# A hybrid decoder layer on one core: the first input row sent together with its norms, block products grouped by tile shape, transposes in place of selecting products, and an output scaled by VectorE alone

## The chip, the cores and the metric

One Trainium2 chip, one core used. The time is device microseconds of one execution of the whole program. The engines run their own instruction streams side by side and wait for one another by semaphores: TensorE (PE for its matmuls, PEld for its weight loads in the profile), VectorE (DVE), ScalarE (ACT), GpSimd (POOL) and SyncE (SP). DMAs are issued by SP, ACT or POOL and carried out by 16 DMA engines that all three share.

## The reference

One step of a decoder layer for 288 tokens: a prompt of 256 and 8 samples of 4. The model width is 2048.

```
h = rms_norm(x, norm1)
z = h @ w_in          # q, k, v of both branches, gates
A: sliding-window attention (128), 16 q heads, 4 kv heads, with a sink
B: gated linear attention, 4 heads, key dim 256, value dim 512:
   prompt: o_t = sum over s <= t of (q_t . decay(s..t) . k_s) v_s, and the final state
   samples: the same, on top of a cached 256x512 state per sample and head
   o = rms_norm(o) * silu(z_r)
y = sigmoid(z_gs) * (o_A @ p_swa) + sigmoid(z_gg) * (o_B @ p_gla)
x = x + y @ w_o
x = x + square(relu(rms_norm(x, norm2) @ w_up)) @ w_down
return rms_norm(x, final_norm), new caches and states
```

## The kernel before, in words

Everything is held with features on the 128 partitions and the 288 tokens along the free axis, so x is 16 rows of 128x288 (a "row" below is one such 128x288 slice, 144 KB). Weights are read once, in chunks of 128x1024 (512 KB, 521 of them), each holding two halves of 128x512. Every product of a weight and an activation is made from three fp32r products of 128x288: high part by high part (L230), high part of the weight by low part of the activation (L231), low part of the weight by high part of the activation (L232). `wsplit` makes the two parts of a weight half: ACT casts it to `whi` (L208), DVE subtracts to get `wlo` (L155). Five `whi` and five `wlo` buffers let this run some two chunks ahead of PE; six `raw` buffers let SP load further ahead. A `gemm` of 512 output columns has four PSUM banks `mm` and runs over 8 chunks, 24 matmuls each.

**The first gemm, `kv`,** is the only one whose activations are made while it runs. `load_x` loads two rows of x per chunk (SP, L266 and L268), then ACT makes `hh` = x times norm1 (L270), DVE the low part `hl` (L271), and the squares of x for the norm are taken by ACT (chunks 1, 3, 5, 6, 7) or by POOL (chunks 0, 2, 4) and added into `acc1` by DVE or POOL (L152). The normalisation itself, `rstd1`, is applied to the gemm's output; `rsqrt_mean` gets it by summing `acc1` over partitions with the matmuls `ssq` (L240), then two ACT and four DVE operations. norm1 is part of the tile `norms` (26 KB), which POOL's queue sends (L166). Ahead of the first real matmul PE runs nine matmuls of 128x512 on a constant tile, `warm` (L302).

**The order of the work** on each engine comes from a scheduler that takes the program as written with its own idea of costs. Generators (`swa`, `gla`, `gla_sample`) are put into queues, and `pump` advances them by some pieces after every weight chunk, so that attention and the linear attention of one head lie between the chunks of the gemms.

**The prompt's linear attention** (`gla`) builds a 256x256 causal score matrix in one PSUM bank, `pa` (diagonal blocks of 128 at columns 0 to 127 and 256 to 383, the off-diagonal block between them). Decays are factored per block, so it is put together from one 128x128 product (`cross`, L652), two of 64x64 (L658), four of 32x32 next to the diagonal (L660) and eight of 32x32 on it (L663), each contracted over 128 partitions and made twice (t = 0 and 1), for each of 4 heads. All operands are f32, and the profile has two MATMUL records for each such product. The 64x64 products both go to PSUM partitions 0 to 63. `at` is the copy of `pa` in SBUF.

**The samples** (`gla_sample`) have their 512 outputs in four partial sums on the four groups of 32 partitions of `ob`. Four products with a 128x32 selecting matrix `ii` (L782) turn them and add the four; ACT copies the result into `og` (L783).

**The end.** After the last gemm, `rsqrt_mean` gives `rstd3`; the 16 rows of x1 are scaled by it in six pieces, four on DVE (1, 3, 4 and 3 rows) and two on POOL (2 and 3 rows) (L149), and sent to `y` by SP and ACT (L968). The two prompt states of the last head, `sp`, are made last (PE L692, ACT copy L694, SP DMA L695).

Of the kernel before, what the change touches and what calls it, by code (L numbers as in the profile page):

```python
# [130 lines left out]
def step_kernel(ctx: ExitStack, tc: tile.TileContext, a: dict):  # L131
# [80 lines left out]
    def gemm(name, xh, xl, evac, rate=(), first=None):  # L212
        nk = 2 * chunks_of(name)
        ps = [pmm.tile([P, 512], F32, name="mm", tag="mm") for _ in range(4)]
        for c in range(nk // 2):
# [2 lines left out]
            raw = main.tile([P, 1024], F32, name="raw", tag="raw", bufs=6)
            if FIRST[name] + c == 0:
                for s in range(2):  # L220
                    SY.dma_start(raw[:, 512 * s:512 * s + 512], a["w"][0, :, 512 * s:512 * s + 512])
# [4 lines left out]
            turns = c in (0, nk // 2 - 1)
            for i, m in [(i, m) for m in range(4) for i in range(2)] if turns else [(i, m) for i in range(2) for m in range(4)]:
                k, hi, lo = parts[i]
                o, sl = ps[m][:, :NT], slice(m * P, m * P + P)
                T.matmul(o, lhsT=hi[:, sl], rhs=xh(k), start=k == 0, stop=False)  # L230
                T.matmul(o, lhsT=hi[:, sl], rhs=xl(k), start=False, stop=False)  # L231
                T.matmul(o, lhsT=lo[:, sl], rhs=xh(k), start=False, stop=k == nk - 1)  # L232
                if k == nk - 1:
# [26 lines left out]
    acc1 = [main.tile([P, NT], F32, name=f"acc1{i}", tag=t) for i, t in ((0, "acc"), (1, "acc_b"))]  # L260

    def load_x(c):
        sl = slice(2 * c, 2 * c + 2)
        if c == 0:
            for k in range(2):
                SY.dma_start(xa[:, k], a["x"][:, k])  # L266
        else:
            SY.dma_start(xa[:, sl], a["x"][:, sl])  # L268
        for k in (2 * c, 2 * c + 1):
            S.mul(hh[:, k], xa[:, k], n1[:, k:k + 1])  # L270
            V.scalar_tensor_tensor(hl[:, k], xa[:, k], n1[:, k:k + 1], f(hh[:, k]), ALU.mult, ALU.subtract)  # L271
        sq = early.tile([P, 2, NT], F32, name="sq", tag="sq", bufs=3)
        odd = c in (1, 3, 5, 6, 7)
        if odd:
            S.activation(flat(sq), flat(xa[:, sl]), AF.Square)
# [292 lines left out]
    def gla(h):  # L568
# [36 lines left out]
        V.memset(pa[:, :384], 0.0)  # L605
        kds = []
        for t in range(2):
# [45 lines left out]
            if t == 0:  # L653
                cross()
            for blk in range(2):
                b0 = 256 * blk
# [1 line left out]
                T.matmul(pa[0:64, b0 + 64:b0 + P], lhsT=l64[:, 0:64], rhs=l64[:, 64:P], start=False, stop=False)  # L658
                for i in (0, 64):
                    T.matmul(pa[i:i + 32, b0 + i + 32:b0 + i + 64], lhsT=l32[:, i:i + 32],  # L660
                             rhs=l32[:, i + 32:i + 64], start=False, stop=False)
                for i in (0, 32, 64, 96):
                    T.matmul(pa[i:i + 32, b0 + i:b0 + i + 32], lhsT=en[:, blk, i:i + 32],  # L663
                             rhs=dg[:, i:i + 32], start=False, stop=False)
# [25 lines left out]
        def state(t, pst, tag="A"):  # L690
# [4 lines left out]
            SY.dma_start(a["sp"][h, t], so)  # L695
# [9 lines left out]
    def gla_sample(h):  # L705
# [75 lines left out]
        for j in range(4):  # L781
            T.matmul(pt[:, TS * j:TS * j + TS], lhsT=ob[:, P * j:P * j + P], rhs=ii, start=True, stop=True)  # L782
# [268 lines left out]
```

## Time and profile before

| | |
|---|---|
| runs | 1806.95, 1806.47, 1808.19 us (median 1806.95) |
| profiled execution: time, span | 1806.9 us, 1805.1 us |
| mean granted TensorE clock | 0.998 |
| PE, PEld, DVE, ACT, POOL busy | 1789.4, 1746.8, 1103.2, 855.8, 84.6 us |
| HBM read, written | 298.25 MB, 23.66 MB |

The span runs from the first to the last instruction of the profiled execution; 1.8 us of its time lie around it. "Busy" counts the time in which at least one instruction of the engine was in flight. Since matmuls are pipelined, neighbouring records overlap, and the pace of PE is read from the distance between the starts of two matmuls. A row of the timeline has start, duration, engine, line, operation, tiles, form and count, and in brackets the idle time ahead of it with what ended it.

### The profile page before, as it was taken

The numbers are of one execution on the slowest core, as the hardware profiler recorded it, in microseconds if no ns is written. First come the engines' busy times: TensorE is split into PE (matmuls) and PEld (weight loads), VectorE is DVE, ScalarE is ACT, GpSimd is POOL, SyncE is SP. The second block draws the span as 40 slices with busy tenths as digits, with TensorE's granted clock in tenths as the row PEclk, the third lists the DMA queues.
The fourth block names the chain that finished last, engine by engine and source line by source line (L and its number), as shares of the span: only waits on it lengthen the run. The fifth ranks groups of instructions, "written<-read, shape, count | busy, mean of one in ns | idle before, by whom it ended". The sixth has DMA issues, their size and how long they took to land.

```text
span 1805.1 us, 34198 instructions
## 1 busy us (share of the span) xinstructions
PE 1789.4 (99%) x13499; PEld 1746.8 (97%) x13499; DVE 1103.2 (61%) x2092; ACT 855.8 (47%) x1593; POOL 84.6 (5%) x97
## 2 busy tenths in 40 slices
PE   9999999999999999999999999999999999999997
PEld 8999998998999989999999999999999999999997
DVE  7886575685665767666666554455544554455544
ACT  5566464443453644554444553345433553345443
POOL 2000000100100101000123000000000000000002
PEclk9999999999999999999999999999999999999999
DMA  7734347557557466545554444544444444444452
GB/s 270 242 120 164 131 153 260 201 188 251 176 205 260 137 248 223 167 168 168 206 176 164 164 166 161 175 164 164 163 168 167 168 161 167 164 167 169 156 175 88
DMA packets 92177, 324.13 MB, mean 180 GB/s; under 512 B 11040, under 2 KB 12720, under 8 KB 92016
## 3 DMA queue, kind: packets, MB, share of 16 engines
q1 hardware_dynamic: 91584, 320.93, 51.1%
q8 instruction: 106, 1.74, 0.4%
q10 hardware_dynamic: 288, 0.74, 0.1%
q0 software_dynamic: 144, 0.28, 0.1%
q14 instruction: 55, 0.45, 0.1%
HBM read 298.25 MB, written 23.66 MB: 178 GB/s over the span
## 4 chain that ended last, share of the span: by engine, by line
PE 96%; DVE 2%; ACT 1%; issue 0%; DMA 0%; DVEq 0%; SPq 0%; ACTq 0%
PE mm L230 30%; PE mm L232 30%; PE mm L231 30%; PE pu L771 1%; PE pos L762 1%; DVE wlo L155 1%; PE pst L692 1%; PE score L379 0%; PE po L685 0%; DMA raw<-in_w 0%; PE pt L408 0%; PE ssq L240 0%; PE o L418 0%; DVE x L149 0%; ACT whi L208 0%
## 5 line engine op out<-in xcount | busy, mean ns | idle before, releaser
L155 DVE TENSOR_TENSOR wlo<-raw,whi 128x512 fp32r<-128x512 f32 x1040 | 721.4, 705 | 601.1 <-ACT whi L208 599.2
L208 ACT CAST whi<-raw 128x512 fp32r<-128x512 f32 x1040 | 631.7, 619 | 832.5 <-PE mm L231 782.0
L230 PE MATMUL mm<-hh,whi 128*128 128x288 f32 x1472 | 441.2, 300 | 1.2 <-ACT whi L208 0.6
L232 PE MATMUL mm<-hh,wlo 128*128 128x288 f32 x1472 | 434.1, 295 | 2.0 <-DVE wlo L155 1.8
L231 PE MATMUL mm<-hl,whi 128*128 128x288 f32 x1472 | 434.3, 295 | 0.0
L232 PE MATMUL mm<-h2h,wlo 128*128 128x288 f32 x1024 | 301.9, 295 | 0.0
L232 PE MATMUL mm<-uh,wlo 128*128 128x288 f32 x1024 | 301.9, 295 | 0.0
L230 PE MATMUL mm<-h2h,whi 128*128 128x288 f32 x1024 | 301.8, 295 | 0.0
L230 PE MATMUL mm<-uh,whi 128*128 128x288 f32 x1024 | 301.8, 295 | 0.0
L231 PE MATMUL mm<-h2l,whi 128*128 128x288 f32 x1024 | 301.6, 295 | 0.0
L231 PE MATMUL mm<-ul,whi 128*128 128x288 f32 x1024 | 301.6, 295 | 0.0
L230 PEld LDWEIGHTS mm<-hh,whi 128*128 128x128 f32 x1472 | 277.1, 188 | 6.0 <-issue 1.7
L232 PEld LDWEIGHTS mm<-hh,wlo 128*128 128x128 f32 x1472 | 276.8, 188 | 3.0 <-DVE wlo L155 2.7
L231 PEld LDWEIGHTS mm<-hl,whi 128*128 128x128 f32 x1472 | 277.2, 188 | 2.6 <-issue 0.7
L232 PEld LDWEIGHTS mm<-h2h,wlo 128*128 128x128 f32 x1024 | 192.3, 188 | 0.0
L232 PEld LDWEIGHTS mm<-uh,wlo 128*128 128x128 f32 x1024 | 192.3, 188 | 0.0
L231 PEld LDWEIGHTS mm<-ul,whi 128*128 128x128 f32 x1024 | 192.1, 188 | 0.1
L231 PEld LDWEIGHTS mm<-h2l,whi 128*128 128x128 f32 x1024 | 192.1, 188 | 0.1
L230 PEld LDWEIGHTS mm<-uh,whi 128*128 128x128 f32 x1024 | 192.0, 188 | 0.1
L230 PEld LDWEIGHTS mm<-h2h,whi 128*128 128x128 f32 x1024 | 192.0, 188 | 0.1
L232 PE MATMUL mm<-yh,wlo 128*128 128x288 f32 x256 | 75.5, 295 | 0.0
L232 PE MATMUL mm<-gh,wlo 128*128 128x288 f32 x256 | 75.4, 295 | 0.0
(274 smaller groups left out, 1823.0 us busy)
## 6 DMA issues: line engine op xcount, KB each, us to landing
raw<-in_w SPq DMA_DIRECT2D x519, 512.0 KB, 3.3
raw<-in_s SPq DMA_DIRECT2D x32, 512.0 KB, 3.7
out_ssn<-raw SPq DMA_DIRECT2D x32, 512.0 KB, 2.9
x<-in_x SPq DMA_DIRECT2D x4, 576.0 KB, 6.1
out_sp<-so SPq DMA_DIRECT2D x8, 256.0 KB, 2.7
x<-in_x SPq DMA_DIRECT2D x7, 288.0 KB, 8.1
kc<-in_kc SPq DMA_DIRECT2D x2, 512.0 KB, 7.0
out_kcn<-kc SPq DMA_DIRECT2D x2, 512.0 KB, 5.5
```

What stands on the lines that cost most here:

```text
L155: eng.tensor_tensor(out, x, y, ALU.subtract)
L208: S.copy(hi, raw)
L230: T.matmul(o, lhsT=hi[:, sl], rhs=xh(k), start=k == 0, stop=False)
L231: T.matmul(o, lhsT=hi[:, sl], rhs=xl(k), start=False, stop=False)
L232: T.matmul(o, lhsT=lo[:, sl], rhs=xh(k), start=False, stop=k == nk - 1)
L692: T.matmul(pst, lhsT=kdt[:, blk, P * t:P * t + P], rhs=vt[:, blk], start=blk == 0, stop=blk == 1)
L762: T.matmul(pos[r:r + 32], lhsT=qm[:, t, 32 * (b0 + g):32 * (b0 + g) + 32], rhs=st[g][:, 512 * t:512 * t + 512], start=b0 == 0, stop=b0 == ...
L771: T.matmul(pu, lhsT=km[:, P * t:P * t + P], rhs=vs, start=True, stop=True)
```

## The change

Five things change.

1. **norm1 travels with the first row of x.** A new tile `xn` (norm1 and row 0) is the first DMA of SP, row 1 the second. The first weight chunk is issued in two halves by ACT, ahead of its table load. The other constants (`norms` without norm1, `ident`, `bm`, `seg`) leave POOL's queue for SP's, behind the loads of the first gemm. In chunk 1 each row and each weight half is a DMA of its own.
2. **Order inside the first gemm.** ACT and DVE now treat each half of a chunk by itself: `hh`, `whi`, `hh`, `whi`, and the squares behind them. All squares are ACT's, all sums DVE's (one addition of 128x576 for each chunk but the first, whose squares are written to `acc1` directly); POOL does nothing there. PE takes the first half of chunk 0 as four high, four low-activation and four low-weight products instead of switching between both halves.
3. **Block products grouped by tile shape.** Both 64x64 products come first, the second one now on PSUM partitions 64 to 127 at columns 384 to 447 of `pa`; then the eight 32x32 on the diagonal, then the four beside it. A second, small ACT copy brings the moved block to its place in `at`; the memset of `pa` covers 448 columns.
4. **Transposes for the samples.** The four products with `ii` become four 128x128 transposes, and DVE adds the four partial sums with one reduction of 128x512 out of PSUM, in place of ACT's copy.
5. **The end.** The two `sp` copies and their DMAs (now on ACT's queue) are written ahead of the scaling; DVE alone scales x1, in ten pieces of 1, 1, 2, 2, 2, 2, 2, 2, 1 and 1 rows, and SP sends each.

```
-    G.dma_start(norms, a["norms"])
+    raw0 = main.tile([P, 1024], F32, name="raw", tag="raw", bufs=6)
+    for s in range(2):
+        S.dma_start(raw0[:, 512 * s:512 * s + 512], a["w"][0, :, 512 * s:512 * s + 512])
...
+            parts = []
+            for s in range(2):
+                if first is not None:
+                    first[1](2 * c + s)
+                parts.append((2 * c + s, *wsplit(raw[:, 512 * s:512 * s + 512])))
             if first is not None:
-                first(c)
...
+                first[2](c)
-            turns = c in (0, nk // 2 - 1)
+            turns = c == nk // 2 - 1 or c == 0 and first is None
...
+            if c == 0 and first is not None:
+                order[:12] = [(0, m, j) for j in range(3) for m in range(4)]
...
+    def weigh_x(k):
+        n1 = xn[0][:, k:k + 1]
+        S.mul(hh[:, k], x_row(k), n1)
+        V.scalar_tensor_tensor(hl[:, k], x_row(k), n1, f(hh[:, k]), ALU.mult, ALU.subtract)
+    def square_x(c):
         if c == 0:
+            acc1.append(early.tile([P, 2, NT], F32, name="acc1"))
             for k in range(2):
+                S.activation(acc1[0][:, k], x_row(k), AF.Square)
         else:
-        odd = c in (1, 3, 5, 6, 7)
-        if odd:
-            S.activation(flat(sq), flat(xa[:, sl]), AF.Square)
-        else:
-            mul(sq, xa[:, sl], xa[:, sl], G)
-        e, acc = (V, acc1[1]) if odd else (G, acc1[0])
...
+            S.activation(flat(sq), flat(xa[:, 2 * c:2 * c + 2]), AF.Square)
+            add(flat(acc1[0]), flat(acc1[0]), flat(sq))
...
+        xn.append(early.tile([P, KT + NT], F32, name="xn"))
+        SY.dma_start(xn[0], a["xn"])
+        SY.dma_start(xa[:, 1], a["x"][:, 1])
...
-    G.dma_start(ident, a["ident"])
-    G.dma_start(bm, a["bm"])
-    G.dma_start(seg, a["seg"])
+    SY.dma_start(norms, a["norms"])
+    SY.dma_start(ident, a["ident"])
+    SY.dma_start(bm, a["bm"])
+    SY.dma_start(seg, a["seg"])
...
-            for blk in range(2):
-                b0 = 256 * blk
-                l64, l32, dg = e[:, 2 + blk], e[:, 7 + blk], e[:, 4 + blk]
-                T.matmul(pa[0:64, b0 + 64:b0 + P], lhsT=l64[:, 0:64], rhs=l64[:, 64:P], start=False, stop=False)
-                for i in (0, 64): ...
-                for i in (0, 32, 64, 96): ...
+            for r, c in ((0, 64), (64, 384)):
+                l64 = e[:, 2 + r // 64]
+                T.matmul(pa[r:r + 64, c:c + 64], lhsT=l64[:, 0:64], rhs=l64[:, 64:P], start=False, stop=False)
+            for blk in range(2):
+                for i in (0, 32, 64, 96): ...
+            for blk in range(2):
+                for i in (0, 64): ...
...
         S.copy(at, pa[:, :384])
+        S.copy(at[0:64, 320:384], pa[64:P, 384:448])
...
-            T.matmul(pt[:, TS * j:TS * j + TS], lhsT=ob[:, P * j:P * j + P], rhs=ii, start=True, stop=True)
-        S.copy(o_g[:, :, TP:NT], pt[:, :4 * TS].rearrange("p (a b) -> p a b", a=4))
+            T.transpose(pt[:, P * j:P * j + P], ob[:, P * j:P * j + P], ident)
+        V.tensor_reduce(o_g[:, :, TP:NT], pt.rearrange("p (a b c) -> p a c b", a=4, b=4), AX.X, ALU.add)
...
-    for sl, e, q in ((slice(0, 1), V, SY), (slice(11, 13), G, S), (slice(1, 4), V, SY), (slice(4, 8), V, SY),
-                     (slice(13, 16), G, S), (slice(8, 11), V, SY)):
...
     for t in range(2):
-        final[0](t, pmm.tile([P, 512], F32, name="mm", tag="mm"), "AF"[t])
+        final[0](t, pmm.tile([P, 512], F32, name="mm", tag="mm"), "AF"[t], S)
+    i = 0
+    for n in (1, 1, 2, 2, 2, 2, 2, 2, 1, 1):
+        sl = slice(i, i + n)
+        mul(x1[:, sl], x1[:, sl], rstd3.unsqueeze(1).broadcast_to([P, n, NT]))
+        SY.dma_start(a["y"][:, sl], x1[:, sl])
+        i += n
```

PE, head 0, t = 0, where the block products stand (rows with `pa`; `pos` and `pu` behind them belong to the samples). Before:

```order
L652 MATMUL pa<-e 128x128
L658 MATMUL pa<-e 64x64
L660 MATMUL pa<-e 32x32 x2
L663 MATMUL pa<-e,en 32x32 x4
L658 MATMUL pa<-e 64x64
L660 MATMUL pa<-e 32x32 x2
L663 MATMUL pa<-e,en 32x32 x4
L762 MATMUL pos<-raw,qm 32x512 x4
```

The same place now:

```order
L678 MATMUL pa<-e 128x128
L684 MATMUL pa<-e 64x64 x2
L688 MATMUL pa<-e,en 32x32 x8
L693 MATMUL pa<-e 32x32 x4
L793 MATMUL pos<-raw,qm 32x512 x4
```

The products are the same in number; the run of 64x64 shapes is one instead of two.

DVE in chunks 1 and 2 of the first gemm. Before:

```order
L271 SCALAR_TENSOR_TENSOR hl<-x,norms,hh 128x288 x2
L152 TENSOR_TENSOR acc_83<-sq 128x288
L155 TENSOR_TENSOR wlo<-raw,whi 128x512 x2
L271 SCALAR_TENSOR_TENSOR hl<-x,norms,hh 128x288 x2
L155 TENSOR_TENSOR wlo<-raw,whi 128x512 x2
```

Now, in chunk 1:

```order
L291 SCALAR_TENSOR_TENSOR hl<-x,xn,hh 128x288
L155 TENSOR_TENSOR wlo<-raw,whi 128x512
L291 SCALAR_TENSOR_TENSOR hl<-x,xn,hh 128x288
L155 TENSOR_TENSOR wlo<-raw,whi 128x512
L152 TENSOR_TENSOR acc_121<-acc_121,sq 128x576
```

`hl` and `wlo` alternate by halves, and from chunk 1 on every chunk ends with one addition on DVE.

DVE's last rows. Before:

```order
L255 SCALAR_TENSOR_TENSOR rstd_11818<-rs_t,rstd_11818 128x288
L149 TENSOR_TENSOR x_10604<-x_10604,rstd_11818 128x288
L149 TENSOR_TENSOR x_10604<-x_10604,rstd_11818 128x864
L149 TENSOR_TENSOR x_10604<-x_10604,rstd_11818 128x1152
L149 TENSOR_TENSOR x_10604<-x_10604,rstd_11818 128x864
L1027 UNCONDITIONAL_BRANCH
```

Now:

```order
L268 SCALAR_TENSOR_TENSOR rstd_11817<-rs_t,rstd_11817 128x288
L149 TENSOR_TENSOR x_10603<-x_10603,rstd_11817 128x288 x2
L149 TENSOR_TENSOR x_10603<-x_10603,rstd_11817 128x576 x6
L149 TENSOR_TENSOR x_10603<-x_10603,rstd_11817 128x288 x2
L1060 UNCONDITIONAL_BRANCH
```

DVE has 16 rows in ten pieces instead of 11 in four. One more move, which the lists of PE show: the 32 matmuls `ag` of the low-rank gate stood directly behind the last matmul of the first gemm, and now stand behind the first 26 matmuls of the next gemm, `q0`.

More of the change, by code (lines that the diff above doesn't have):

```diff
@@ L158, in step_kernel @@
     ident = main.tile([P, P], F32, name="ident")
-    norms = main.tile([P, 52], F32, name="norms")
+    norms = main.tile([P, 36], F32, name="norms")
     ones = main.tile([P, P], F32, name="ones")
@@ L215, in gemm @@
         for c in range(nk // 2):
-            if first is not None:
-                first(c)
[L218 to L221, printed above, removed]
-            else:
-                SY.dma_start(raw, a["w"][FIRST[name] + c])
-            parts = [(2 * c + s, *wsplit(raw[:, 512 * s:512 * s + 512])) for s in range(2)]
-            turns = c in (0, nk // 2 - 1)
-            for i, m in [(i, m) for m in range(4) for i in range(2)] if turns else [(i, m) for i in range(2) for m in range(4)]:
+            if FIRST[name] + c == 0:
+                raw = raw0
+            else:
+                raw = main.tile([P, 1024], F32, name="raw", tag="raw", bufs=6)
+                if first is not None:
+                    first[0](c, raw)
+                else:
+                    SY.dma_start(raw, a["w"][FIRST[name] + c])
+            parts = []
+            for s in range(2):
+                if first is not None:
+                    first[1](2 * c + s)
+                parts.append((2 * c + s, *wsplit(raw[:, 512 * s:512 * s + 512])))
+            if first is not None:
+                first[2](c)
+            turns = c == nk // 2 - 1 or c == 0 and first is None
+            order = [(i, m) for m in range(4) for i in range(2)] if turns else [(i, m) for i in range(2) for m in range(4)]
+            order = [(i, m, j) for i, m in order for j in range(3)]
+            if c == 0 and first is not None:
+                order[:12] = [(0, m, j) for j in range(3) for m in range(4)]
+            for i, m, j in order:
                 k, hi, lo = parts[i]
                 o, sl = ps[m][:, :NT], slice(m * P, m * P + P)
[L230 to L233, printed above, removed]
+                T.matmul(o, lhsT=(lo if j == 2 else hi)[:, sl], rhs=xl(k) if j == 1 else xh(k),
+                         start=k == 0 and j == 0, stop=k == nk - 1 and j == 2)
+                if k == nk - 1 and j == 2:
                     evac(m, o)
@@ L604, in gla @@
         pa = bank("pa")
-        V.memset(pa[:, :384], 0.0)
+        V.memset(pa[:, :448], 0.0)
         kds = []
@@ L694, in state @@
             S.copy(so, pst)
-            SY.dma_start(a["sp"][h, t], so)
+            q.dma_start(a["sp"][h, t], so)
         done.add(h)
```

56 lines of the change are left out of this document (28 added, 28 removed).

## The prediction

> **What bounds the kernel.** I read the page first (busy shares, chain), then what PE waits for, then the timeline of the three places that the change touches. Busy shares and chain:
>
> ```profile
> PE 1789.4 (99%) x13499; PEld 1746.8 (97%) x13499; DVE 1103.2 (61%) x2092; ACT 855.8 (47%) x1593; POOL 84.6 (5%) x97
> PE 96%; DVE 2%; ACT 1%; issue 0%; DMA 0%; DVEq 0%; SPq 0%; ACTq 0%
> ```
>
> The waits of PE (engine and line, releaser, us in total, times, longest), but for the one for its first operand:
>
> ```profile
> PE mm L232 <- DVE wlo L155: 1.8, 2, 1.0
> ...
> PE mm L230 <- DVE ya L149: 1.0, 2, 0.6
> PE mm L230 <- ACT whi L208: 0.6, 1, 0.6
> ```
>
> PE is the bound from its first matmul to its last: it waits 3.4 us in all, 2.4 of them in the first gemm. So time can come from three sources only: the start, where PE waits and runs slowly; PE's own work; and the tail behind its last matmul, where DVE, POOL and DMA end the span. What only loads DVE, ACT or SP in between is covered by PE. The sum is made against the profiled execution (1806.9 us), which stands 0.05 under the median of the runs (1806.95).
>
> **The start.** Timeline of the first 38 us:
>
> ```profile
> 1.68 4.02 PE L302 MATMUL warm<-warm 128*128 128x512 bf16 x9 [1.68 <-DVE warm L299]
> 4.82 0.96 ACT L270 ACTIVATE hh<-x,norms 128x288 fp32r<-128x288 f32 x2 [2.73 <-DMA norms<-in_norms]
> 6.34 0.61 PE L230 MATMUL mm<-hh,whi 128*128 128x288 f32 x1 [0.64 <-ACT whi L208]
> 9.71 1.14 ACT L208 CAST whi<-raw 128x512 fp32r<-128x512 f32 x2
> 10.11 0.43 PE L230 MATMUL mm<-hh,whi 128*128 128x288 f32 x1
> 10.35 0.33 PE L231 MATMUL mm<-hl,whi 128*128 128x288 f32 x1
> 10.65 0.29 PE L230 MATMUL mm<-hh,whi 128*128 128x288 f32 x1
> 10.78 0.29 PE L231 MATMUL mm<-hl,whi 128*128 128x288 f32 x1
> 12.53 2.06 DVE L271 SCALAR_TENSOR_TENSOR hl<-x,norms,hh 128x288 fp32r<-128x288 f32 x2
> 13.66 0.67 ACT L275 ACTIVATE sq<-x 128x576 f32<-128x576 f32 x1
> 14.51 2.85 DVE L155 TENSOR_TENSOR wlo<-raw,whi 128x512 fp32r<-128x512 f32 x2
> 16.89 2.12 POOL L152 TENSOR_TENSOR acc<-acc,sq 128x288 f32<-128x288 f32 x2
> 19.61 0.68 DVE L155 TENSOR_TENSOR wlo<-raw,whi 128x512 fp32r<-128x512 f32 x1
> 21.19 0.93 DVE L271 SCALAR_TENSOR_TENSOR hl<-x,norms,hh 128x288 fp32r<-128x288 f32 x2
> 22.05 1.28 DVE L155 TENSOR_TENSOR wlo<-raw,whi 128x512 fp32r<-128x512 f32 x2
> 37.06 0.30 PE L515 MATMUL ag<-hh,wr 128*128 128x288 f32 x1
> ```
>
> ACT waits 2.73 us for norms; PE starts 0.64 us after the warm matmuls. Its matmuls start 0.24 us apart (10.11 to 10.35) until 10.3, and 0.133 from then on. From 12.5 to 19 DVE takes twice as long for the same forms (two `hl` 2.06 against 0.93, two `wlo` 2.85 against 1.28), just while POOL works on the squares. The gemm, 192 matmuls by 0.133 and about 1.0 us for the four f32 records of `ssq`, should take 26.5 us; it took 37.06 - 6.34 = 30.7. So 4.2 us are lost: some 17 slow matmuls by 0.107, 1.8 us, and 2.4 in stalls behind DVE.
>
> *Earlier start.* Size and time to landing:
>
> ```profile
> x<-in_x SPq DMA_DIRECT2D x2, 144.0 KB, 2.3
> raw<-in_w SPq DMA_DIRECT2D x2, 256.0 KB, 3.9
> ```
>
> `xn` is one x row and 64 bytes more a partition, and SP's first DMA (at 0.8 us, where SP begins): it lands at 3.1 to 3.5. The weight half, issued by ACT at the same time, lands by 0.8 + 3.9 = 4.7 (the 3.9 stood behind two x loads); ACT casts it in 0.6, so the first matmul is ready by 5.3. The warm matmuls hold PE until 1.68 + 9 x 0.427 (512 columns at the pace of 288 in 0.24) = 5.53. PE goes on there without a gap: -0.8 us. If the half came a microsecond later, 0; the row it is nearest to says not.
>
> *Stalls behind DVE.* Without POOL a chunk costs DVE 0.93 + 1.28 + one 128x576 addition, about 0.75 (288 take 0.47, 512 take 0.68): 2.96. ACT needs 0.96 + 1.14 + 0.67 = 2.8, PE 24 x 0.133 = 3.2. Both keep up: -2.4 us; at worst half of it, if chunks come late.
>
> *Slow matmuls.* If the slow stretch ends at 10.3 as before, the earlier start puts 0.8 us more work into it: +0.3. If it ends 3.9 us after unbroken work begins, as it did after the gap (6.34 to 10.3), the warm matmuls use it up: -1.8. I take -1.1, nearer to the second end, since the gap is the only interruption and it goes. [...]
>
> *New waits behind the gemm.* `ag`, which covered the wait for `rstd1`, now stands behind 26 matmuls of `q0`, whose first needs a bank that the evacuation of `kv` frees. `ssq` stands 24 matmuls (3.2 us) before that. The same chain in the tail takes 1793.87 - 1791.38 = 2.5 us (rows below) to the first use, and the use 0.47: 3.0. One `wlo` may stand in its way. So 0 to 0.7 us; I take +0.2. `ag` itself needs `wr` 3.4 us later, behind two `wlo` and a cast: nothing.
>
> Start: -0.8 - 2.4 - 1.1 + 0.2 = -4.1 (ends -5.0 and -1.0).
>
> **PE's own work.** The block products of head 0, t = 0, up to the second L658, and the duration of the 32-wide records (min/median/max ns):
>
> ```profile
> 260.79 0.33 PE L658 MATMUL pa<-e 128*64 128x64 f32 x2
> 261.05 0.22 PE L660 MATMUL pa<-e 128*32 128x32 f32 x2
> 261.12 0.25 PE L663 MATMUL pa<-e,en 128*32 128x32 f32 x6
> 261.30 0.33 PE L658 MATMUL pa<-e 128*64 128x64 f32 x2
> L663 PE MATMUL pa<-e,en x128: 196/196/217, 261.1 to 645.7; 128*32 128x32 f32 x128
> ```
>
> The pair of L658 holds PE for 0.26 us, the twelve 32-wide records for 0.25. But these twelve start between 261.05 and 261.17 (the last ends at 261.37 and lasts 0.196): products on different column groups run side by side, and 0.13 then pass before the next shape starts. Now one round of 0.51 goes from each of 8 stretches (4 heads, two t), and what moves into the other round costs 0.12 for its twelve records and 0 to 0.13 (half of 0.26) for the second 64x64 product, beside the first one on other column groups or behind it: 0.51 - 0.12 - 0 to 0.13 = 0.26 to 0.39, eight times -2.1 to -3.1. I take -2.8, nearer to side by side, as the 32-wide ones go. [...]
>
> Transposes: the four products with `ii`, and four transposes of the new form, each with the next matmul:
>
> ```profile
> 335.82 0.97 PE L782 MATMUL pt<-bm,ob 128*128 128x32 f32 x8
> 336.63 0.38 PE L230 MATMUL mm<-hh,whi 128*128 128x288 f32 x1
> ...
> 245.29 0.60 PE L599 MATMUL pv<-ident,zv 128*128 128x128 f32 x4
> 245.65 0.38 PE L230 MATMUL mm<-hh,whi 128*128 128x288 f32 x1
> ```
>
> 0.81 us to the next matmul against 0.36: four heads by 0.45, -1.8 us (ends -1.6 and -1.9). DVE's reduction of 512 elements costs about 0.7 (0.68 for `wlo`) in place of a short ACT copy; four of them, like the second `at` copy, the wider memset and the constants on SP's queue, lie under PE, which sees DVE 61% busy; without that cover they would be 3 us.
>
> **The tail.** Timeline, busy time by microsecond (last two columns: DMA share, GB/s), and the DMA of 1793 to 1805.1:
>
> ```profile
> 1791.38 0.50 ACT L250 ACTIVATE rs_t<-ssq,epst 128x288 f32<-128x288 f32 x1 [1.00 <-PE ssq L240]
> 1793.87 6.67 DVE L149 TENSOR_TENSOR x<-x,rstd 128x288 f32<-128x288 f32 x4
> 1793.98 4.37 POOL L149 TENSOR_TENSOR x<-x,rstd 128x576 f32<-128x576 f32 x2 [3.01 <-DVE rstd L255]
> 1800.99 0.41 SPq L695 DMA_DIRECT2D out_sp<-so  x1
> ...
> 1794.00:1795.00 1.00, 0.77 (x2) 0.00 (x0) 1.00 (x2) 0.00 (x0) 1.00 (x1) 1.00 0.44 168
> 1802.00:1803.00 1.00, 0.00 (x0) 0.00 (x0) 0.00 (x0) 0.00 (x0) 0.00 (x0) 0.50 1.02 406
> 1803.00:1804.00 1.00, 0.00 (x0) 0.00 (x0) 0.00 (x0) 0.00 (x0) 0.00 (x0) 0.50 0.66 250
> ...
> DMA packets 1152, 2.88 MB, mean 238 GB/s; under 512 B 128, under 2 KB 256, under 8 KB 1152
> ```
>
> DVE scales 11 rows in 6.67 us beside POOL (slowed as at the start) and ends at 1800.54; the last `sp` is issued at 1801, behind all of `y`, though its products are long done. Alone, DVE needs 0.36 us for a row and 0.66 for two (0.93 for two `hl`, 1.28 for two `wlo`, less overlap): 4 x 0.36 + 6 x 0.66 = 5.4, done at 1799.3. Then DMA is the limit: 2.88 MB at 400 GB/s are 7.2 us from 1794.6 (0.44 of that microsecond used), so 1801.8, against 1803.65 before. I take -1.6, since it won't be full at once (ends -0.3, if only the last `sp` moves, and -2.0).
>
> **Sum.** -4.1 - 2.8 - 1.8 - 1.6 = -10.3: 1806.9 - 10.3 = 1796.6 us. All best ends: -5.0 - 3.1 - 1.9 - 2.0 = -12.0, 1794.9; all worst: -1.0 - 2.1 - 1.6 - 0.3 = -5.0, 1801.9.
>
> **Rivals.** (a) *The start gives a third:* the slow stretch stays (+0.3) and half the stalls too, since x, weights and `xn` share the DMA engines from two queues: -0.8 - 1.2 + 0.3 + 0.2 = -1.5, total 1799.2. For it: 3.9 us for 256 KB; against it: PE needs chunk 2 at some 12 us only. (b) *Grouping gives nothing,* as a change of column group waits as well: 1799.4. Against it: twelve starts in 0.12 us. (c) *The tail stays,* ten small DMAs costing what POOL's absence saves: 1798.2. [...] (d) *Slower:* DVE's slowness from 12 to 19 us comes from the loads, not from POOL. Then DVE, with POOL's sums, needs 2.06 + 2.85 + 1.5 = 6.4 us a chunk against PE's 3.2 while loads run, some 6 chunks: +19 and none of the 2.4, in all 1818. It decides where two `wlo` without POOL still take over 2.4 us. Against it: the `wlo` of 0.68 at 19.61, behind POOL's last sum with the loads still running.
>
> **Chances.** Forecast 0.70, (a) 0.12, (b) 0.06, (c) 0.09, (d) 0.03. 0.2% is 3.6 us, about what a measurement of this kernel tells from no change; all but (d) lie further below, and only (a), (b) and (c) together come within it: faster 0.95, same 0.03, slower 0.02. Range 1793.8 to 1800.4: the cases (a) to (c) one at a time, the best end, and about 1 us for the spread of runs.
>
> **What would show it.** `hh` at about 3.3 with no wait for norms; no gap between `warm` and the first `mm`; no PE wait for `wlo` before 30 us, pairs of `wlo` at 1.28; one 64-wide run in each stretch; 0.36 us for four transposes; DVE's last scaling 5.5 us after its first, DMA full from 1796 on. I am wrong if PE waits microseconds for the evacuation behind `rstd1`, if the pace of 0.24 lasts to 10 us, or if the last landing still comes 10 us after the scaling begins.

## The result, and the profile after

| | before | after |
|---|---|---|
| median of the runs | 1806.8 us (1806.47 to 1808.19) | 1797.0 us (1795.73 to 1797.18) |
| profiled execution: time, span | 1806.9, 1805.1 us | 1795.7, 1794.0 us |
| first matmul of the first gemm | 6.34 us | 5.19 us |
| its last matmul (192nd) | 36.93 us | 31.57 us |
| first scaling of x1 to the last landing | 10.25 us | 8.67 us |

The ratio is 0.9943 (95% interval 0.9931 to 0.9955), 9.8 us by the medians, 11.2 us between the two profiled executions. Busy shares and chain of the changed kernel:

```profile
PE 1782.1 (99%) x13483; PEld 1741.2 (97%) x13483; DVE 1104.9 (62%) x2100; ACT 856.7 (48%) x1597; POOL 71.0 (4%) x83
PE 96%; DVE 2%; ACT 1%; issue 0%; DMA 0%; DVEq 0%; ACTq 0%
```

The bound is the same engine; it ends 9.4 us earlier. What PE still waits for, but for its first operand (engine and line, releaser: us in all, times, longest):

```profile
PE mm L244 <- DVE ya L149: 1.0, 2, 0.6
PE pu L802 <- ACT og L718: 0.4, 1, 0.4
```

Both waits for `wlo` and the one for `whi` are gone; a wait of `pu` is new. The start, from the timeline (start, duration, engine, line, operation; in brackets the idle time ahead and what ended it):

```profile
1.67 3.69 PE L327 MATMUL warm<-warm 128*128 128x512 bf16 x9 [1.67 <-DVE warm L324]
4.09 0.54 ACT L290 ACTIVATE hh<-xn 128x288 fp32r<-128x288 f32 x1 [1.08 <-DMA xn<-in_xn]
4.54 0.60 ACT L211 CAST whi<-raw 128x512 fp32r<-128x512 f32 x1
5.19 0.79 PE L244 MATMUL mm<-hh,whi 128*128 128x288 f32 x4
5.82 0.69 PE L244 MATMUL mm<-hl,whi 128*128 128x288 f32 x4
```

PE goes from the warm matmuls into the gemm without a gap, and from the second matmul on its starts lie 0.13 us apart: there is no slow stretch at all. DVE's work in the stretch of 8 to 22 us, grouped by form (busy us, mean ns of one):

```profile
L155 DVE TENSOR_TENSOR wlo<-raw,whi 128x512 fp32r<-128x512 f32 x11 | 7.5, 686 | 0.2 <-ACT whi L211 0.2
L291 DVE SCALAR_TENSOR_TENSOR hl<-x,xn,hh 128x288 fp32r<-128x288 f32 x10 | 5.1, 512 | 0.0
L152 DVE TENSOR_TENSOR acc<-acc,sq 128x576 f32<-128x576 f32 x5 | 3.8, 751 | 0.0
```

Every `wlo` takes 0.69 us there, where two took 2.85 before. The block products of head 0, t = 0, and one group of transposes with the matmul behind it:

```profile
255.72 0.34 PE L684 MATMUL pa<-e 128*64 128x64 f32 x4
255.99 0.33 PE L688 MATMUL pa<-e,en 128*32 128x32 f32 x16
...
330.02 0.60 PE L813 MATMUL pt<-ident,ob 128*128 128x128 f32 x4
330.38 0.38 PE L244 MATMUL mm<-hh,whi 128*128 128x288 f32 x1
```

Four 64-wide records now hold PE for 0.27 us, as two did. The tail in the timeline:

```profile
1784.50 5.57 DVE L149 TENSOR_TENSOR x<-x,rstd 128x288 f32<-128x288 f32 x10
```

And its busy time by microsecond (length of the stretch; busy time and instructions of PE, PEld, DVE, ACT, POOL; granted TensorE clock; DMA share; GB/s):

```profile
1786.00:1787.00 1.00, 0.00 (x0) 0.00 (x0) 1.00 (x2) 0.09 (x1) 0.00 (x0) 1.00 0.85 302
1787.00:1788.00 1.00, 0.00 (x0) 0.00 (x0) 1.00 (x3) 0.00 (x0) 0.00 (x0) 1.00 1.03 404
...
1792.00:1793.00 1.00, 0.00 (x0) 0.00 (x0) 0.00 (x0) 0.00 (x0) 0.00 (x0) 0.50 0.73 258
```

DVE scales all 16 rows in 5.57 us, less than it took for 11 beside POOL; the DMA engines are full from 2.5 us after the first scaling until all bytes are out.

### The profile page after: what moved, and what is told of

It reads as the page before. It is cut to its first block, busy times and chain, and to the rows that moved or that the text cites. A ratio compares the mean times of both kernels' runs of the same rounds, so it can differ in the third digit from the quotient of the medians.

```text
span 1794.0 us, 34188 instructions
## 1 busy us (share of the span) xinstructions
PE 1782.1 (99%) x13483; PEld 1741.2 (97%) x13483; DVE 1104.9 (62%) x2100; ACT 856.7 (48%) x1597; POOL 71.0 (4%) x83
## 3 DMA queue, kind: packets, MB, share of 16 engines
q8 instruction: 105, 1.72, 0.4%
## 4 chain that ended last, share of the span: by engine, by line
PE 96%; DVE 2%; ACT 1%; issue 0%; DMA 0%; DVEq 0%; ACTq 0%
PE mm L244 90%; PE pu L802 1%; PE pos L793 1%; PE pst L723 1%; PE score L405 0%; DVE wlo L155 0%; PE pt L434 0%; DVE x L149 0%; PE po L716 0%; PE ssq L253 0%; ACT whi L211 0%; PE o L444 0%; DMA raw<-in_w 0%; PE warm L327 0%; DVE og L833 0%
```

## The experiments

My theory after the two traces: POOL's two-input work slowed DVE at the start and in the tail; the early start, the pace of PE, the blocks and the transposes each add what their rows show. Each run below traced one execution. The rivals: loads slowed DVE; the pace is chance; shape changes alone, or side-by-side running alone, make the gain of the blocks; the order of `sp` makes that of the tail. All runs in one table, with the median of the kernel before on the same chip, and four points of the first gemm in each trace (us; "full pace" is where the distance of two starts falls to half):

| kernel | median | before | ratio (95%) | first matmul | full pace | 97th | 192nd |
|---|---|---|---|---|---|---|---|
| before | | | | 6.34 | 10.4 | 23.37 | 36.93 |
| after | 1797.0 | 1806.8 | 0.9943 (0.9931 to 0.9955) | 5.19 | 4.9 | 18.01 | 31.57 |
| after_again | 1796.2 | 1806.9 | 0.9941 (0.9929 to 0.9954) | 5.26 | 5.6 | 18.28 | 31.85 |
| warm6 | 1798.1 | 1806.9 | 0.9949 (0.9936 to 0.9963) | 5.32 | 10.9 | 20.63 | 34.19 |
| before_warm14 | 1808.2 | 1806.9 | 1.0008 (0.9999 to 1.0017) | 7.05 | 6.8 | 24.02 | 37.58 |
| pool_two | 1805.3 | 1806.9 | 0.9990 (0.9981 to 0.9999) | 5.21 | 4.8 | 27.30 | 40.86 |
| norm1_sp | 1797.5 | 1807.0 | 0.9947 (0.9933 to 0.9961) | 6.61 | 5.0 | 19.43 | 33.00 |
| side_big | 1797.6 | 1807.0 | 0.9947 (0.9934 to 0.9961) | 5.23 | 5.0 | 18.05 | 31.62 |
| pool_one_tail | 1802.0 | 1807.0 | 0.9971 (0.9959 to 0.9982) | 5.29 | 6.4 | 21.36 | 35.09 |
| before_nopool | 1804.9 | 1807.0 | 0.9989 (0.9980 to 0.9998) | 7.28 | 5.3 | 20.11 | 33.67 |
| halves_sp | 1797.8 | 1807.2 | 0.9953 (0.9938 to 0.9968) | 7.07 | 5.5 to 7.1 | 19.88 | 33.45 |
| best | 1795.1 | 1807.2 | 0.9935 (0.9922 to 0.9947) | 5.04 | 5.5 | 18.48 | 32.04 |

**after_again.** No edit.

> The changed kernel once more, unaltered. If the moment at which TensorE's full pace begins is set by the unbroken work that leads up to it, it comes again 3.1 to 3.3 us after the first warm matmul (near 4.9 us), the first gemm has no matmul at the pace of 0.24 us, and the median lies within 0.5 us of 1795.7. [...] Blocks (0.85 and 0.89 us a stretch), transposes (0.49 us) and the tail (8.7 us from the first scaling to the last landing) are to come out the same to 0.05 us, the tail to 0.3.

Full pace came 0.7 us later than in the first trace (5.6 us), one matmul was slow, and the gemm ended 0.28 us later: the moment does vary, though by little here. Blocks, transposes and the tail (8.67 us) came out the same to 0.01 us. Single times went from 1795.85 to 1797.32.

**warm6.** A break ahead of the gemm.

```
-        for i in range(9):
+        for i in range(6):
             T.matmul(warm, ...)
```

> The changed kernel with 6 warm matmuls in place of 9: they end at 1.67 + 6 x 0.427 = 4.23 us, and PE then stands still for about 1.0 us until the first weight half is cast (5.19 us). If a break delays the full pace, as the trace of the kernel before suggested (0.64 us of break, full pace 4.1 us after the first matmul of the gemm), it begins between 8.4 and 9.3 us, 13 to 17 matmuls take 0.24 us, and the time is 1.4 to 1.8 us above the changed kernel. Rival: only the time since the first matmul counts; then the full pace is there at 4.9 us in spite of the break, and the time is that of the changed kernel within 0.3 us.

Timeline of its PE:

```profile
5.32 1.33 PE L244 MATMUL mm<-hh,whi 128*128 128x288 f32 x4 [0.90 <-ACT whi L211]
10.52 0.45 PE L244 MATMUL mm<-hh,whi 128*128 128x288 f32 x1
11.09 0.29 PE L244 MATMUL mm<-hh,whi 128*128 128x288 f32 x1
```

The slow matmuls (0.45 us each, 0.24 apart) last until 10.9 us, later than I expected, and the gemm ends 2.6 us after that of the changed kernel (34.19 against 31.57). The rival, time since the first matmul, falls; PE's busy time ahead of the full pace, which came even later than forecast, is in the last section. Of this profiled execution 2.6 us are waits of `pu` (below), against 0.4 in the changed kernel, so its whole time says less than the gemm.

**before_warm14.** The kernel before, without the break.

```
-        for i in range(9):
+        for i in range(14):
             T.matmul(warm, ...)
```

> The kernel before with 14 warm matmuls in place of 9, so that PE has no break ahead of the first gemm. If the break is what delayed the full pace there, it now begins during the warm matmuls (near 4.9 us, at the latest 8.1), the first gemm starts between 6.3 and 7.0 us with few or no slow matmuls, and the time is 1.0 to 1.8 us below the kernel before. Rival: the full pace waits for something else in that start (the loads, the order of the products), and begins at 10.4 us as before; then the longer warm-up only delays the first matmul, from 6.34 to 7.66 us, with fewer slow ones behind it (12 in place of 17): 0.7 us above the kernel before.

A row of PE's timeline:

```profile
12.67 0.40 PE L232 MATMUL mm<-hh,wlo 128*128 128x288 f32 x1 [1.11 <-DVE wlo L155]
```

Busy time in the windows between three changes of pace (columns as above):

```profile
6.85:10.26 3.41, 3.41 (x26) 3.27 (x25) 1.47 (x4) 1.33 (x3) 0.00 (x0) 1.00 0.97 385
10.26:13.67 3.41, 1.86 (x12) 1.39 (x11) 3.31 (x4) 3.41 (x8) 2.67 (x3) 1.00 1.03 406
13.67:17.08 3.41, 3.41 (x16) 3.41 (x15) 3.41 (x4) 3.05 (x7) 3.25 (x4) 0.50 1.03 401
```

The mechanism came as forecast: full pace from 6.85 us, inside the warm matmuls. The gain did not. PE did 24 matmuls by 11 us, ran ahead of DVE, which was late beside POOL, waited 1.11 us for `wlo`, and then lost its full pace again for exactly one stretch of 3.41 us (clock 0.50). At the 97th matmul and at the 192nd it was 0.65 us behind the kernel before; a wait of 1.7 us of `pu`, much later, makes up the rest of what this execution lost. A faster PE was worth nothing here in front of a late DVE; my prediction counted the two as independent terms.

**pool_two.** Two-input work on POOL again, its results unused, with nothing else changed.

```
             S.activation(flat(sq), flat(xa[:, 2 * c:2 * c + 2]), AF.Square)
+            if c < 6:
+                dm = early.tile([P, 2, NT], F32, name="dm", tag="dm")
+                for _ in range(2):
+                    mul(flat(dm), flat(xa[:, ...]), flat(xa[:, ...]), G)
```

> The changed kernel, in which POOL besides multiplies x by x ten times (128x576, two per chunk in chunks 1 to 5 of the first gemm) into a tile that nobody reads. If POOL's two-input work is what halved DVE's speed in the kernel before, two wlo take about 2.8 us in place of 1.28 and two hl 2.0 in place of 0.93 while POOL works, for 14 to 20 us; DVE then makes about half of the 2.96 us of work per chunk in the 3.2 us that PE takes for it, and PE waits 4 to 7 us in all for wlo: 4 to 7 us above the changed kernel. Rival: the loads slowed DVE, and the new order of the loads cured it; then nothing changes, wlo pairs stay at 1.28 to 1.4 us and the time within 0.5 us of the changed kernel.

DVE and POOL from 8 to 22 us, grouped by form:

```profile
L155 DVE TENSOR_TENSOR wlo<-raw,whi 128x512 fp32r<-128x512 f32 x4 | 6.5, 1630 | 0.2 <-ACT whi L211 0.2
L291 DVE SCALAR_TENSOR_TENSOR hl<-x,xn,hh 128x288 fp32r<-128x288 f32 x4 | 5.6, 1397 | 0.0
L152 DVE TENSOR_TENSOR acc<-acc,sq 128x576 f32<-128x576 f32 x2 | 3.4, 1699 | 0.0
...
L149 POOL TENSOR_TENSOR dm<-x 128x576 f32<-128x576 f32 x10 | 13.9, 1386 | 8.1 <-DMA x<-in_x 7.4
```

What PE waits for in the gemm:

```profile
PE mm L244 <- DVE wlo L155: 3.7, 4, 1.2
PE mm L244 <- DVE hl L291: 1.2, 1, 1.2
```

Busy time in four windows of 3.41 us, counted back from the last change of pace:

```profile
11.64:15.05 3.41, 1.73 (x11) 1.50 (x11) 3.41 (x3) 3.41 (x8) 3.25 (x3) 1.00 1.04 418
15.05:18.47 3.42, 1.83 (x12) 1.62 (x13) 3.42 (x4) 1.35 (x3) 3.19 (x4) 1.00 1.03 415
18.47:21.88 3.41, 2.63 (x12) 2.28 (x11) 3.41 (x3) 1.63 (x3) 3.25 (x3) 0.50 0.80 269
21.88:25.29 3.41, 3.41 (x13) 2.81 (x12) 3.41 (x6) 1.06 (x2) 0.61 (x1) 0.50 0.19 74
```

`wlo` went from 686 to 1630 ns, `hl` from 512 to 1397, the sum from 751 to 1699, with the loads and their order unchanged: 2.3 to 2.7 times, but nearly the same addition for each, 0.94, 0.89 and 0.95 us. The rival "loads" falls. The gemm was 9.3 us longer, more than the 4 to 7 expected: 4.9 us are waits for DVE, and behind the stalls PE ran without its full pace for two stretches of 3.41 us (clock 0.50 from 18.47 to 25.29).

**norm1_sp.** norm1 apart from row 0 again, and the last `sp` behind `y`.

```
-        SY.dma_start(xn[0], a["xn"])
+        G.dma_start(n1t[0], a["xn"][:, :KT])
+        SY.dma_start(xn[0][:, KT:], a["xn"][:, KT:])
...
-    for t in range(2):
-        final[0](t, ..., "AF"[t], S)
     (the ten pieces of y)
+    for t in range(2):
+        final[0](t, ..., "AF"[t], SY)
```

> Two undone parts of the changed kernel that lie 1780 us apart, each read in its own stretch. Start: norm1 is a DMA of its own on POOL's queue again (row 0 stays SP's first DMA). It landed at 4.80 us in the kernel before; then hh starts at 4.8 in place of 4.1 and the first matmul at 5.9 to 6.0, behind a break of 0.4 to 0.7 us. If any break delays the full pace, it comes near 10 us with some 15 slow matmuls: 0.7 + 1.6 = 2.3 us above the changed kernel by the 96th matmul of the gemm. Rival: the pace, once freed during the warm matmuls, outlives so short a break: 0.7 us. Tail: the second sp is sent by SP behind all pieces of y. If the bytes bound the tail, its length from the first scaling to the last landing stays 8.7 us (at most +0.3); if the place of the last sp counts, as I allowed with the end of -0.3 us for moving it alone, it is some 1 us longer.

The first `hh` and the first matmuls in the timeline:

```profile
5.51 0.53 ACT L290 ACTIVATE hh<-xn,n1t 128x288 fp32r<-128x288 f32 x1 [2.50 <-DMA n1t<-in_xn]
6.61 0.80 PE L244 MATMUL mm<-hh,whi 128*128 128x288 f32 x4 [1.19 <-ACT whi L211]
```

norm1 landed at 5.49 us, later than in the kernel before (4.80); the two weight halves are now issued beside it, as beside `xn`, which landed at 4.1 us with them (the changed kernel) and at 3.1 without (halves_sp). The first matmul came at 6.61, and the gemm stayed 1.43 us behind: the rival was right, full pace (5.0 us) outlived a break of 1.2 us. The tail was 8.62 us with `sp` issued last, at 6.3 us after the first scaling: its place costs nothing here, where bytes bound the tail.

**halves_sp.** The other part of the start undone.

```
-    for s in range(2):
-        S.dma_start(raw0[:, 512 * s:512 * s + 512], a["w"][0, ...])
...
         SY.dma_start(xa[:, 1], a["x"][:, 1])
+        for s in range(2): SY.dma_start(raw0[:, 512 * s:512 * s + 512], a["w"][0, ...])
```

> The changed kernel with the two halves of the first weight chunk issued by SP, behind xn and row 1, as in the kernel before. There the first half, issued at 1.73 us, landed at 5.45; then its cast ends near 6.1 us and the first matmul starts at 6.1 to 6.2, 0.9 us later than in the changed kernel, although norm1 is there in time. If the pace has been freed during the warm matmuls (it was in five of the seven starts with nine of them that I have seen), the gemm stays 0.9 us later; if not, up to 1.8 us more. Rival: it is norm1 alone that set the start; then the half lands no later than 4.7 us, with less competition at that moment, and the first matmul starts by 5.4.

The same place in the timeline of this kernel:

```profile
3.14 0.53 ACT L290 ACTIVATE hh<-xn 128x288 fp32r<-128x288 f32 x1 [1.05 <-DMA xn<-in_xn]
6.40 1.32 ACT L211 CAST whi<-raw 128x512 fp32r<-128x512 f32 x2 [1.64 <-DMA raw<-in_w]
7.07 0.79 PE L244 MATMUL mm<-hh,whi 128*128 128x288 f32 x4 [1.37 <-ACT whi L211]
```

The first half, issued at 1.72 us, landed at 6.37, though it landed at 5.45 in the kernel before, where it was issued at 1.73; why, the runs do not show. So PE began at 7.07 instead of the 6.1 to 6.2 that I expected, 1.9 us later than in the changed kernel and 0.7 later than before. With the weights out of the way `xn` landed at 3.1 us, as I had forecast for the change itself. So neither part alone starts PE earlier: norm1 with row 0 alone starts it at 7.07, the halves on ACT's queue alone at 6.61, both together at 5.19. By the medians the two runs are 0.5 to 1.5 us slower than the changed kernel, with overlapping intervals.

**side_big.** Both 64x64 products on the same partitions, and five larger pieces of `y`.

```
-            for r, c in ((0, 64), (64, 384)):
+            for r, c in ((0, 64), (64, 320)):
                 l64 = e[:, 2 + r // 64]
-                T.matmul(pa[r:r + 64, c:c + 64], ...)
+                T.matmul(pa[0:64, c:c + 64], ...)
...
-    for n in (1, 1, 2, 2, 2, 2, 2, 2, 1, 1):
+    for n in (1, 3, 4, 4, 4):
```

> Two undone parts, read each in its own stretch. Blocks: still grouped by shape, but the second 64x64 product goes to partitions 0 to 63 as in the kernel before (no second copy to at). If the two products gain by running side by side on different column groups, the four 64-wide records take 0.39 to 0.52 us in place of 0.265, and each of the 8 stretches is 0.13 to 0.26 us longer, 1.0 to 2.1 us in all. Rival: only the number of shape changes counts; then the stretches stay at 0.852 and 0.891 us. Tail: DVE alone scales in five pieces of 1, 3, 4, 4 and 4 rows. If bytes bound the tail, it stays within 0.3 us of 8.7 us; if a larger piece is dearer because its first byte waits for its last element, up to 0.8 us longer; if small DMAs cost (the rival of the ten pieces), up to 0.5 us shorter.

The block products of head 0, t = 0, in the timeline:

```profile
255.70 0.45 PE L684 MATMUL pa<-e 128*64 128x64 f32 x4
256.08 0.33 PE L688 MATMUL pa<-e,en 128*32 128x32 f32 x16
```

The next shape follows the first 64-wide record after 0.375 us in place of 0.265, and each of the 8 stretches is 0.11 us longer (0.962 and 1.000 against 0.852 and 0.891). Side by side makes 0.11 of the gain of 0.37 a stretch, one run of shapes instead of two the other 0.26. The tail took 8.75 us: five pieces of 144 to 576 KB cost 0.08 us more than ten of 144 to 288 KB.

**pool_one_tail.** POOL at the start with one-input operations; the old scaling in the tail.

```
+            if c < 6:
+                dm = early.tile([P, 2, NT], F32, name="dm", tag="dm")
+                for _ in range(2):
+                    G.tensor_scalar(flat(dm), flat(xa[:, ...]), 2.0, 1.0, ALU.mult, ALU.mult)
...
-    (the ten pieces of y)
+    (the six pieces of the kernel before, behind sp)
```

> Two additions to the changed kernel, each read in its own stretch. Start: POOL works in chunks 1 to 5 of the first gemm as in the run with ten multiplications, but on operations with one input (x times 2, 128x576, ten of them). If any work of POOL slows DVE, wlo is at 1.4 to 1.6 us and the gemm about 9 us longer, as there; if it takes POOL's second input, wlo stays at 0.69, hl at 0.51, and the gemm's length within 0.3 us of the changed kernel. I expect the second, with chance 0.6. Tail: the scaling of the kernel before (DVE 11 rows in four pieces, POOL 5 rows in two, sent by SP and ACT), but with the copies and DMAs of sp ahead. If POOL's share is what made the old tail long, DVE takes 6.7 us for its 11 rows and the tail is 9.6 to 10.2 us from the first scaling to the last landing; if it was the late sp, the tail is 8.7 us as in the changed kernel.

DVE from 8 to 22 us, grouped by form:

```profile
L155 DVE TENSOR_TENSOR wlo<-raw,whi 128x512 fp32r<-128x512 f32 x8 | 7.8, 971 | 0.0
L291 DVE SCALAR_TENSOR_TENSOR hl<-x,xn,hh 128x288 fp32r<-128x288 f32 x8 | 5.6, 702 | 0.3 <-ACT hh L290 0.3
```

A `wlo` beside POOL, and the tail's scaling, in the timeline:

```profile
8.10 1.15 DVE L155 TENSOR_TENSOR wlo<-raw,whi 128x512 fp32r<-128x512 f32 x1
...
1788.84 6.67 DVE L149 TENSOR_TENSOR x<-x,rstd 128x288 f32<-128x288 f32 x4
1788.96 4.37 POOL L149 TENSOR_TENSOR x<-x,rstd 128x576 f32<-128x576 f32 x2 [3.01 <-DVE rstd L268]
```

I had expected no effect of one-input work, and was wrong: `wlo` is at 971 ns on average, 1.15 us where it lies beside POOL (1.7 times the 0.69 of POOL idle), and the gemm ends 3.5 us later (0.5 of it slow matmuls: full pace only at 6.4 us). The tail is 10.10 us. The last `sp` was issued 4.9 us after the first scaling, not 7.1 as in the kernel before, and that changed the end by 0.15 us: the old tail was long because of POOL's share.

**before_nopool.** One part of the change alone, in the kernel before.

```
-        if odd:
-            S.activation(flat(sq), flat(xa[:, sl]), AF.Square)
-        else:
-            mul(sq, xa[:, sl], xa[:, sl], G)
-        e, acc = (V, acc1[1]) if odd else (G, acc1[0])
+        S.activation(flat(sq), flat(xa[:, sl]), AF.Square)
+        e, acc = V, acc1[1 if odd else 0]
```

> The kernel before with one part of the change alone: in its first gemm ACT takes all squares and DVE all sums, POOL nothing; the start, its order and the tail stay. If POOL's work made DVE late there, two wlo take 1.28 us throughout, the two waits of PE for wlo (1.10 and 1.34 us between matmuls) go, and the time is 2.0 to 2.8 us below the kernel before. Rival: with 3.1 us of work a chunk (0.93 + 1.28 + two sums of 0.46) DVE stays behind PE's 3.2 us because of late loads; then PE still waits over 1 us for wlo and the gain is under 1 us.

The first matmul in the timeline:

```profile
7.28 0.40 PE L230 MATMUL mm<-hh,whi 128*128 128x288 f32 x1 [1.65 <-ACT whi L208]
```

DVE from 8 to 22 us, grouped by form:

```profile
L155 DVE TENSOR_TENSOR wlo<-raw,whi 128x512 fp32r<-128x512 f32 x10 | 6.8, 684 | 0.3 <-ACT whi L208 0.3
```

No wait for `wlo` is left, and `wlo` takes 684 ns throughout. PE began 0.94 us later: `hh` began 0.37 later, norms having landed later, and ACT now has a square ahead of the first cast. It still ended the gemm 3.26 us earlier: 2.4 us of stalls, and 1.8 of slow matmuls, since in this execution full pace came during the warm matmuls. But 0.8 of that went again just behind the gemm, where `ag` now waits for DVE's split of its weight `wr`, a wait that the kernel before does not have:

```profile
PE ag L515 <- DVE wr L155: 0.6, 1, 0.6
```

That leaves 2.4 us for this execution. By the medians about 2 us were gained, with an interval from 0.4 to 3.6: about a fifth of the change's gain.

**best.** Three additions to the changed kernel.

```
-        S.mul(hh[:, k], x_row(k), n1)
+        V.tensor_scalar(hh[:, k], x_row(k), n1, None, ALU.mult) if k == 0 else S.mul(...)
...
-        wt = early.tile([P, 512], ...)
+        wt = early.tile([P, P], ...)
-            T.matmul(warm, lhsT=wt[:, :P], rhs=wt, ...)
+            T.matmul(warm, lhsT=wt, rhs=wt.unsqueeze(1).broadcast_to([P, 4, P]), ...)
...
-            S.copy(o_g[:, 2 * jj:2 * jj + 2, 0:TP], po...)
+            V.tensor_copy(o_g[:, 2 * jj:2 * jj + 2, 0:TP], po...)
```

> The changed kernel with three small additions: DVE instead of ACT makes the first row of hh, so that ACT casts the first weight half at once; the warm tile is a 128x128 one, filled first, so that the warm matmuls start near 1.3 us in place of 1.67; and DVE instead of ACT copies po into og, so that pu does not wait for ACT where a weight chunk comes late (0.2 to 2.1 us in the runs of the changed kernel so far). The first matmul should start at 4.9 to 5.0 us, the waits of pu for og should go, and the time be 0.5 to 1.2 us below the changed kernel: 1795.0 to 1795.7. Rival: DVE is late then, either for hl in chunk 0 or for wlo behind the copies, and PE waits as long for it as it gains: no difference beyond 0.3 us.

What PE waits for, but for its first operand:

```profile
PE mm L244 <- DVE ya L149: 1.0, 2, 0.6
```

The wait of `pu` is gone. The start gained 0.15 us and lost more: full pace came at 5.5 us, and PE stopped twice for `wlo`, about 0.2 us each with the restart, so the gemm ended 0.47 us behind the changed kernel's trace. At 1795.1 us the median is 1.1 and 1.9 us below the two medians of the changed kernel, but the intervals of the ratios overlap: it is better by its trace (no wait left in the heads), not by a difference that these runs resolve.

## Why the prediction was right, step by step

Forecast 1796.6 us, measured 1797.0. The terms, read from the two profiled executions at points that both share:

| term | forecast (ends) | measured |
|---|---|---|
| earlier start | -0.8 (-0.8 to 0) | -1.15 |
| slow matmuls | -1.1 (-1.8 to +0.3) | -1.82 |
| stalls behind DVE | -2.4 (-2.4 to -1.2) | -2.39 |
| new waits behind the gemm | +0.2 (0 to +0.7) | +0.23 |
| block products | -2.8 (-3.1 to -2.1) | -2.96 (8 times 0.37) |
| transposes | -1.8 (-1.9 to -1.6) | -1.80 (4 times 0.45) |
| tail | -1.6 (-2.0 to -0.3) | -1.58 to the last landing, -1.77 to the end |
| wait of `pu`, not foreseen | | +0.37 |
| sum | -10.3 | -11.1 of span (0.2 lie in pieces too small to name) |

*Earlier start.* The size is near, the path was not mine. I said that `hh` would begin at 3.3 us without a wait for norm1. It began at 4.09 and waited 1.08 us for `xn`: the weight halves that ACT issues at the same moment share the engines with it, and halves_sp shows the 3.1 us that I had taken for granted. PE started earlier than forecast all the same, because the half landed at 4.27 us, not 4.7, and the warm matmuls ended at 5.2, not 5.53, full pace having come inside them.

*Slow matmuls.* That the break delayed the full pace held (warm6); that 3.9 us of unbroken work bring it did not, and the size was off, 1.82 for 1.1. In four traces the moments at which the pace changed lie multiples of 3.41 us apart (last section); the first of them differs between executions, also of one kernel (4.9 us in after, 5.6 in after_again). The full pace came between 4.8 and 6.8 us in ten of the twelve starts traced, and at 10.4 and 10.9 in the two where PE stood idle for 0.64 and 0.90 us before it. Four of the ten lie at 4.8 to 5.0 us; ahead of the full pace PE had been busy for 3.14 us in pool_two and for 3.22 in the changed kernel. The profiled execution had one of the best moments, which is luck, and can be part of why it lies 1.3 us below the median of its kernel; the other executions have no trace that would show it.

*The terms were not independent.* I added 1.1 for the pace to 2.4 for the stalls. before_warm14 shows the first alone to be worth nothing (its gemm ended 0.65 us later than before), as long as POOL slows DVE; before_nopool shows that with POOL gone both are there. The sum was right only because the change makes all its parts at once; the same holds for the two parts of the start. Had one part been left out of the change, my sum would have been wrong. My lower end for the start, -1.0, also counts the 0.8 of an earlier start that I had allowed to be nothing; without it and the 0.3 that hangs on it, that end is 0 - 1.2 + 0.7 = -0.5.

*Blocks.* I took 0.35 us a stretch for "side by side"; it is 0.37, of which the second product's other partitions make 0.11. Rival (b), a change of column group that waits, falls.

*Tail.* Both numbers came within 0.2 us: DVE's scaling 5.57 against 5.4, the last landing 1.58 us sooner against 1.6. The DMA engines were full some 0.4 us later than forecast (2.5 us after the first scaling, not 2.1). Rival (c), ten small DMAs, falls by the 8.67 us and by side_big: 8.75 us with five.

*Rivals (a) and (d)* fall by the waits of PE and by `wlo` at 0.69 us: no stall is left in the first gemm, though the loads fill the DMA engines (384 to 422 GB/s from 5 to 24 us).

*Not foreseen.* `pu` waits for a PSUM bank that ACT frees by copying `po`, and ACT is behind there when it had to wait for a weight chunk to land: in after, warm6 and before_warm14 it stood idle for 0.27, 2.01 and 1.63 us ahead of a cast 3.6 us earlier, and `pu` then waited 0.36, 2.10 and 1.72, each 0.09 more. It is no part of the change: the same wait is 1.7 us in before_warm14 and none in the kernel before; in the runs built on the changed kernel it was 0.2 to 2.6 us, and none in best, where DVE does the copy. Whether it and the moment of full pace make the 1 to 2 us by which executions of one kernel differ is not shown. Why a chunk lands late in one run and not in another was not tested.

## What to carry to other kernels

Before giving POOL part of an elementwise job, look at the duration of DVE's rows while POOL works: here DVE alone did 16 rows in less time than DVE with POOL's help needed for 11. In a start-up PE begins when the latest of several things is there: price the parts together, and ask for each what is late next, since a faster PE, an earlier norm or earlier weights were each worth nothing alone here. Equal tile shapes in one run, and neighbours on different column groups (here PSUM partitions 0 to 63 and 64 to 127), were worth 0.26 and 0.11 us a time, on a PE that hardly ever waits.

## What the runs showed of the hardware

- **TensorE's pace changed at distances that are multiples of 3.41 us.** In before_warm14 it changed at 6.85, 13.67 and 17.08 us, 6.82 and 3.41 apart; in pool_two at 4.82, 18.47 and 25.29, 13.65 and 6.82 apart: all multiples of 3.41 us to 0.01 us. The clock falls once more behind PE's last matmul, in the kernel before from its first change at 10.403 us to 1798.987, 1788.584 us, in the changed kernel from 4.891 to 1790.062, 1785.171 us. The two differ by 3.413 us; they are 524 and 523 times 3.4133. The last fall in the kernel before and in the changed kernel:

```profile
1798.90:1798.98 0.08, 0.00 (x0) 0.00 (x0) 0.08 (x1) 0.08 (x1) 0.00 (x0) 1.00 0.00 0
1798.99:1799.07 0.08, 0.00 (x0) 0.00 (x0) 0.08 (x1) 0.08 (x1) 0.00 (x0) 0.50 0.00 0
```

```profile
1790.00:1790.05 0.05, 0.00 (x0) 0.00 (x0) 0.05 (x1) 0.00 (x0) 0.00 (x0) 1.00 0.70 276
1790.07:1790.12 0.05, 0.00 (x0) 0.00 (x0) 0.00 (x1) 0.00 (x0) 0.00 (x0) 0.50 0.93 369
```

Counted back from 10.40 us in the kernel before, two stretches of 3.41 us begin at 3.58 and 6.99: the break fell into the first, with PE busy for 2.77 us, and the full pace came at the end of the second, with PE busy for all of it.
- **PE's busy time in the stretch ahead of the full pace.** In the 3.41 us that ended with the full pace PE was busy for as little as 3.08 us (halves_sp), 3.14 (pool_two) and 3.22 (the changed kernel). In 3.41 us counted back in the same way, behind which the pace stayed slow, it was busy for 2.77 (the kernel before), 2.63 (pool_two from 18.47 us on) and 2.51 (warm6). The ends of matmuls in these busy times are modelled, and what a busy time between 2.77 and 3.08 brings is not shown. The kernel before and halves_sp:

```profile
3.58:6.99 3.41, 2.77 (x8) 1.10 (x7) 1.60 (x4) 2.05 (x4) 1.25 (x2) 1.00 1.00 309
2.61:6.02 3.41, 3.08 (x8) 0.80 (x6) 1.04 (x2) 1.62 (x4) 0.00 (x0) 1.00 0.96 251
```

- How idle a stretch must be to lose the full pace is open: with PE busy for 1.83 (pool_two from 15.05 us on) and 1.86 us (before_warm14 from 10.26) of 3.41 it was lost, with 1.73 (pool_two from 11.64 us on) and 1.76 (before_nopool from 5.43) it was not.
- **The clock column does not show the first slow stretch.** It reads 1.00 for 8 to 11 us of the kernel before (the number ahead of the DMA share), while matmuls start 0.24 us apart until 10.4; the later slow stretches it shows as 0.50. The traces of the two kernels hold no clock record ahead of the first change (10.40 and 4.89 us). The window of the kernel before:

```profile
8.00:11.00 3.00, 3.00 (x16) 3.00 (x16) 2.04 (x5) 2.83 (x6) 0.50 (x1) 1.00 1.00 394
```

- **One-input work of POOL slowed DVE too:** `wlo`, 0.69 us with POOL idle, took 1.15 us (1.7 times) beside it in pool_one_tail, against 1.63 (2.4 times) beside two-input work in pool_two.
- **What DVE lost differed with POOL's instruction, and little between DVE's own forms.** Beside POOL's two-input work on 128x576 `wlo`, `hl` and the sum each took 0.89 to 0.95 us longer (pool_two), beside one-input work on 128x576 `wlo` 0.46 and `hl` 0.40 (pool_one_tail: 1.15 for 0.69, 0.91 for 0.51), beside two-input sums of 128x288 `hl` and `wlo` 0.56 to 0.61 (the kernel before: `hl` 1.06 for 0.50, `wlo` 1.29 for 0.68). In pool_two DVE did 10 of these instructions from 8 to 22 us, and POOL 10. Why DVE loses this time is not shown, and the factors above hold for these sizes alone.
